# A third plain group ahead of the Strassen groups in each feed-forward

## The chip, the cores and the metric

One Trainium2 chip, one of its cores. The metric is device time in microseconds (us) of one launch, the median of several runs. Engines are named as in the profile: PE (TensorE, the matmuls; PEld is its weight load), DVE (VectorE), ACT (ScalarE), POOL (GpSimd), SP (the queue from which most DMAs are issued).

## The reference, cut to what matters

A step of a two-layer backbone on 640 tokens (512 latent, 128 context) of width 1024. Each layer has two SwiGLU feed-forwards around a token mixer, so there are four feed-forwards in all:

```python
def swiglu(h, w_in, w_out):          # w_in: 1024 x 5632, w_out: 2816 x 1024
    g, u = jnp.split(h @ w_in, 2, axis=-1)
    return (jax.nn.silu(g) * u) @ w_out
...
    for i in range(DEPTH):           # DEPTH = 2
        h = modulate(rms_norm(x, norm_g[i, 0]), mod[:, 0], mod[:, 1])
        x = x + 0.5 * mod[:, 2] * swiglu(h, ffn_w_in[i, 0], ffn_w_out[i, 0])
        ...                          # token mixer
        h = modulate(rms_norm(x, norm_g[i, 2]), mod[:, 6], mod[:, 7])
        x = x + 0.5 * mod[:, 8] * swiglu(h, ffn_w_in[i, 1], ffn_w_out[i, 1])
```

All data are float32. The change concerns only how `h @ w_in` is computed.

## The kernel before, in words

**Precision.** A float32 product is made of three PE matmuls in a reduced float32 format: each operand is split into a high part `hi` (an ACT copy) and a low part `lo` (a DVE subtraction), and PE adds hi*hi, hi*lo and lo*hi in PSUM. In `mm3x` these are lines 695, 696 and 697, each 128x128 weights by 320 columns, that is half of the 640 tokens (`HT`).

**Feed-forward.** The 22 column groups of `w_in` (128 gate and 128 up columns each, one weight tile `raw` of 1 MB) are worked through in three chunks of 6, 8 and 8 groups; after each chunk the second product (`out_proj`) adds its part to `x`. Groups are numbered from 0. Groups 0 and 1 are *plain*: 2 column blocks x 2 token halves x 8 blocks of the inner dimension x 3 = 96 matmuls. From group `NG0` = 2 on, a group is computed by `strassen_in` with the Strassen-Winograd scheme on 2x2 blocks (gate/up, token halves, inner halves): 7 products x 4 x 3 = 84 matmuls.

**What the Strassen groups need besides.** On the weight side, four block sums per group (DVE, lines 289 to 292), and the splits (`split_piece`) of 3.5 tiles' worth of 1024 columns in four pieces, against two pieces of 1024 for a plain group. The S pieces (piece 2 and 3) are split after the sums. On the token side, once per feed-forward, `tbuild`: from the normalised activations, in four pairs of tiles, ACT adds the shift (line 582), DVE makes four block sums (585 to 588), and both split the results into the tiles T (508 on ACT, 509 on DVE): T00 to T03 in the first feed-forward, T20 to T23, T30 to T33 and T50 to T53 in the others, with `ah`, `al`, `bh`, `bl` for the high and low parts. The first product of a Strassen group needs neither S nor T; the second, into the PSUM tile `pg`, needs the S1 block and the T1 part of all four T tiles.

**Start of a feed-forward.** `first_pair` (in the first feed-forward `first_wide`) interleaves groups 0 and 1 with the end of the normalisation, while `tbuild` starts as soon as the last normalised tile is there. Then group 2 follows. Evacuation of a plain group (`fin_half`): per token half a silu on ACT from one PSUM tile (905) and a product on DVE with the other (906), at the end a split (908, 909). A Strassen group has 3 copies on ACT, 3 additions and 2 products on DVE, 2 silus, and the same split.

**Order.** Each engine executes its own rows in the order in which they stand. A list scheduler with priorities sets that order on PE, DVE and ACT; from the first Strassen group on PE keeps the order of the program text (`pe_manual`). Background generators (`tick`) hand out `tbuild`, the splits and the modulation (`ada`) between matmuls. Weights come through a ring of two `raw` tiles, and split pieces through five `whi`/`wlo` buffers; the next weight load is issued when a `raw` tile has been split. A modulation load stands in the same list: four of them ahead of groups 2 to 5 of the first feed-forward, each used by 8 PE products (line 447, 16 matmuls in the trace) into `adaps`, which also takes one of the 8 PSUM tiles.

Of the kernel before, what the change touches and what calls it, by code (L numbers as in the profile page):

```python
# [31 lines left out]
HALVES = ((0, HT), (HT, T))  # L32
SEGS = (((0, HT, 0),), ((HT, TL, 0), (TL, T, 1)))
NS = 47
NG0 = 2
FA = (4, 6, 9, 12, 14, 18)
QD_ = 512
NW = (6, 9)
# [29 lines left out]
def trunk_kernel(  # L68
# [52 lines left out]
    def sbig(name, dt=F32):  # L121
        return ap_.tile([P, T], dt, tag="s", bufs=NS, name=name)

    def stmp(name, dt=F32):
        return ap_.tile([P, T], dt, tag="s", bufs=NS, name=name)
# [5 lines left out]
    def psm(name):  # L131
        return pp.tile([P, 512], F32, tag="b", bufs=8, name=name)
# [18 lines left out]
    def spawn(gen, wait=0):  # L151
        e = [gen, wait]
        bgs.append(e)
        return e
# [40 lines left out]
    for l in range(2):  # L195
        for s in range(2):
            for g in range(KF):
                wtab["fin", l, s, g] = (w_fin[l * 2 + s, g], KD)
                if g >= NG0:
                    stras.add(("fin", l, s, g))  # L200
# [171 lines left out]
    def next_ada():  # L372
        if adae[0] is not None:
            finish(adae[0])
        k = order[st["i"]]
        adae[0] = spawn((ada_v if k[1:] in ADV else ada)(k))
        step(adae[0])
# [5 lines left out]
    def next_group(key):  # L383
        while order[st["i"]][0] == "ada":
            next_ada()
        j = st["i"]
        assert order[j] == key, (order[j], key)
        st["i"] += 1
        return Wt(j)
# [230 lines left out]
    hs = {}  # L620
# [62 lines left out]
    def mm3(o, W, mcol, k, act, hf, start, stop):  # L683
        wh, wl = W.col(k, mcol)
        mm3x(o, wh, wl, *halves(act, hf), start, stop)
# [14 lines left out]
    def mm_fm(o, W, mcol, acts, hf, ks=None):  # L700
        ks = list(range(len(acts))) if ks is None else ks
        for i, k in enumerate(ks):
            mm3(o, W, mcol, k, acts[k], hf, i == 0, i == len(ks) - 1)
# [55 lines left out]
    def first_pair(i, keys, names):  # L759
        if i == 0:  # L760
            yield from first_wide(i, keys, names)
            return
        Ws = [next_group(keys[0])]
        h = hs[i]
        ps = {}
        for hf in range(2):
            if hf == 0:
                for a in range(2):
                    for j in range(2):
                        ps[a, j, 0] = psm(f"{names[a]}{j}0")  # L770
                la[0] = 0
                for k in range(KD):
                    need_h(i, 0, k)
                    for a in range(2):
                        if a == 1 and k == 0:
                            Ws.append(next_group(keys[1]))
                        for j in range(2):
                            mm3(ps[a, j, 0], Ws[a], j, k, h[k], 0, k == 0, k == KD - 1)
                yield ps, 0
            else:  # L780
                for a in range(2):
                    for j in range(2):
                        ps[a, j, 1] = psm(f"{names[a]}{j}1")
                    for k in range(KD):
                        if k == LK:
                            la[0] = 1
                        need_h(i, 1, k)
                        for j in range(2):
                            mm3(ps[a, j, 1], Ws[a], j, k, h[k], 1, k == 0, k == KD - 1)
                    pe_manual(False)  # L790
                    Ws[a].done()
                    yield ps, 1 + a
# [18 lines left out]
    def out_proj(keys, acts, l, gmod, nxt, ks=None):  # L811
        nw = len(keys) if nxt is None else 2
        for gi in range(nw):
            W = next_group(keys[gi])
            for j in range(2):
                for hf in range(2):
                    op_step(keys[gi], W, gi, j, hf, acts, l, gmod, nxt, ks)
                    mid_ada()
            W.done()
        if nw == len(keys):  # L820
            return
        la[0] = 2
        Ws = {}
        end = nxt == len(PHASES)
        for n_, hf in enumerate((1, 0) if end else (0, 1)):
            pe_manual((n_ == 1 or keys[0][0] == "fout") and not end)
            for gi in (2, 3):
                if n_ == 0:
                    Ws[gi] = next_group(keys[gi])
                for j in range(2):  # L830
                    op_step(keys[gi], Ws[gi], gi, j, hf, acts, l, gmod, nxt, ks)
                    mid_ada()
                if n_ == 1:
                    Ws[gi].done()
            chains[nxt, hf] = spawn(norm_chain(nxt, hf, NW[hf]))
# [57 lines left out]
    def ffn(i, l, s, nxt):  # L893
        base = 0
        for ci, n in enumerate(CHUNKS):
            acts = []

            def start_g(g):
                nm = f"a{l}{s}{g}"
                return [sbig(nm + "h", F32R), sbig(nm + "l", F32R), stmp(nm + "s")]  # L900

            def fin_half(e, pg, pu, hf):
                ahi, alo, sg = e
                t0, t1 = HALVES[hf]
                S.activation(out=sg[:, t0:t1], in_=pg[:, :t1 - t0], func=AF.Silu)
                V.tensor_tensor(out=sg[:, t0:t1], in0=sg[:, t0:t1], in1=pu[:, :t1 - t0], op=ALU.mult)
                if hf == 1:
                    S.activation(out=ahi, in_=sg, func=AF.Copy)
                    V.tensor_tensor(out=alo, in0=sg, in1=ahi.bitcast(F32), op=ALU.subtract)

            g0 = base
            if base == 0:
                es = [start_g(0), start_g(1)]
                for ps, stg in first_pair(i, [("fin", l, s, 0), ("fin", l, s, 1)], [f"pf{l}{s}{a}" for a in range(2)]):
                    for a in ((0, 1) if stg == 0 else (stg - 1,)):
                        fin_half(es[a], ps[a, 0, min(stg, 1)], ps[a, 1, min(stg, 1)], min(stg, 1))
                acts += [e[:2] for e in es]
                g0 = 2
            for g in range(g0, base + n):
                e = start_g(g)  # L920
                strassen_in(i, l, s, g, e)
                acts.append(e[:2])
            lastf = nxt if ci == len(CHUNKS) - 1 else None
            if i == 0 and ci == 2:
                spawn(even_tables())
            out_proj([("fout", l, s, ci, g) for g in range(4)], acts, l, 2 if s == 0 else 8, lastf)
            base += n
# [615 lines left out]
    for i, (l, s) in enumerate(PHASES):  # L1543
        if s == 1:
            (even_mixer if l == 0 else odd_mixer)(i, i + 1)
        else:
            ffn(i, l, s // 2, i + 1)
# [108 lines left out]
```

## Time and profile before

| | |
|---|---|
| median of 3 runs | 2505.2 us (2503.99 to 2509.65) |
| the profiled execution's own time | 2501.56 us |
| its span, first to last instruction | 2499.8 us |
| mean granted PE clock | 0.982 of full speed |
| PE busy | 2398.9 us (96% of the span) |
| DVE busy | 1863.5 us (75%) |
| ACT busy | 1077.8 us (43%) |

The profile shows one execution. "Idle before" is the time in which an engine had nothing running ahead of an instruction, with the instruction that released it. [...]

### The profile page before, as it was taken

How to read it: one execution, taken by the hardware profiler on the slowest of the kernel's cores; microseconds unless marked ns; L12 is line 12 of the kernel's file. 1: busy time of each engine (PE TensorE's matmuls, PEld its weight loads, DVE VectorE, ACT ScalarE, POOL GpSimd, SP SyncE). 2: the span in 40 equal slices, each digit the busy share in tenths (PEclk: the TensorE clock that was granted, in tenths of full speed). 3: DMA queues.
4: the chain of work that ended last, by engine and by line, in shares of the span. 5: the costliest groups of instructions: out<-in, count | busy, mean ns of one | idle time of the engine just before them, and what ended most of it. 6: DMA issues, size and time to landing. Idle time of an engine off the chain costs nothing.

```text
span 2499.8 us, 40660 instructions
## 1 busy us (share of the span) xinstructions
PE 2398.9 (96%) x16482; PEld 2341.4 (94%) x16482; DVE 1863.5 (75%) x3785; ACT 1077.8 (43%) x2038; POOL 62.6 (3%) x86
## 2 busy tenths in 40 slices
PE   7899999999899999999999999999999998999998
PEld 6899999899898999999988999999999988999998
DVE  7677767877878777677967786789788877574674
ACT  4525335333326335153542433526767645252452
POOL 1000000000000000000000000001011000000000
PEclk9999999999999999999999999999999999999999
DMA  7342423323241333423224242342111101222121
GB/s 265 114 156 85 150 70 116 135 104 131 71 150 53 129 122 122 152 101 119 85 93 144 102 169 88 116 163 80 41 43 57 54 34 60 76 85 101 68 102 42
DMA packets 44475, 259.30 MB, mean 104 GB/s; under 512 B 5888, under 2 KB 8576, under 8 KB 16768
## 3 DMA queue, kind: packets, MB, share of 16 engines
q1 hardware_dynamic: 41024, 252.37, 28.4%
q8 instruction: 129, 2.11, 0.3%
q0 software_dynamic: 1280, 2.62, 0.3%
q10 hardware_dynamic: 1984, 1.72, 0.2%
q14 instruction: 58, 0.48, 0.1%
HBM read 252.76 MB, written 3.93 MB: 103 GB/s over the span
## 4 chain that ended last, share of the span: by engine, by line
PE 79%; DVE 11%; ACT 3%; DMA 3%; issue 2%; POOL 0%; POOLq 0%; ACTq 0%; DVEq 0%
PE op L696 7%; PE op L697 7%; PE op L695 7%; PE pu L695 7%; PE pu L696 7%; PE pu L697 7%; PE pg L697 4%; PE pg L696 4%; PE pg L695 3%; DVE wlo L309 3%; PE pf L695 2%; PE pf L696 2%; PE pf L697 2%; ACT whi L308 2%; DMA raw<-in_w_fout 1%
## 5 line engine op out<-in xcount | busy, mean ns | idle before, releaser
L309 DVE TENSOR_TENSOR wlo<-raw,whi 128x1024 fp32r<-128x1024 f32 (+1 forms) x488 | 536.1, 1116 | 282.5 <-ACT whi L308 281.4
L308 ACT ACTIVATE whi<-raw 128x1024 fp32r<-128x1024 f32 (+1 forms) x492 | 471.0, 974 | 632.5 <-DMA raw<-in_w_fout 147.8
L807 DVE SCALAR_TENSOR_TENSOR xs<-op,mod,xs 128x128 f32<-128x128 f32 (+2 forms) x312 | 127.1, 436 | 136.9 <-PE op L697 136.5
L524 ACT ACTIVATE nq<-xs 128x320 f32<-128x320 f32 x84 | 39.1, 468 | 132.2 <-DVE xs L807 130.6
L404 DVE SCALAR_TENSOR_TENSOR raw<-raw,sb 128x1024 f32<-128x1024 f32 x72 | 87.6, 1222 | 0.5
L406 DVE CUSTOM_DVE_ANT_0 raw<-raw,sb 128x1024 f32<-128x1024 f32 x72 | 87.5, 1219 | 0.7
L695 PE MATMUL oq<-H4h,whi 128*128 128x320 f32 x256 | 81.1, 318 | 0.2 <-ACT ov L967 0.2
L697 PE MATMUL oq<-H4h,wlo 128*128 128x320 f32 x256 | 79.6, 311 | 0.0
L696 PE MATMUL oq<-H4l,whi 128*128 128x320 f32 x256 | 79.3, 310 | 0.0
L1304 DVE TENSOR_REDUCE amx<-as 128x1 f32<-128x320 f32 x144 | 61.6, 461 | 19.1 <-PE as L1300 18.8
L1312 ACT ACTIVATE ap<-as,anm 128x320 f32<-128x320 f32 x128 | 66.1, 530 | 14.1 <-DVE anm L1307 13.9
L871 ACT COPY p<-pg 128x320 f32<-128x320 f32 x80 | 34.1, 426 | 64.0 <-PE pg L697 63.9
L291 DVE TENSOR_TENSOR raw<-raw 128x512 f32<-128x512 f32 x80 | 55.2, 690 | 1.9
L289 DVE TENSOR_TENSOR raw<-raw 128x512 f32<-128x512 f32 x80 | 55.2, 689 | 1.8
L290 DVE TENSOR_TENSOR raw<-raw 128x512 f32<-128x512 f32 x80 | 54.8, 685 | 0.8
L292 DVE TENSOR_TENSOR raw<-raw 128x512 f32<-128x512 f32 x80 | 54.8, 685 | 0.6
L695 PEld LDWEIGHTS oq<-H4h,whi 128*128 128x128 f32 x256 | 48.1, 188 | 1.3 <-ACT ov L967 0.5
L696 PEld LDWEIGHTS oq<-H4l,whi 128*128 128x128 f32 x256 | 48.1, 188 | 0.4 <-DVE H4l L614 0.3
L697 PEld LDWEIGHTS oq<-H4h,wlo 128*128 128x128 f32 x256 | 48.1, 188 | 0.0
L528 DVE TENSOR_TENSOR nq<-nq,nq 128x320 f32<-128x320 f32 x82 | 40.1, 491 | 9.6 <-ACT nq L524 9.1
L696 PE MATMUL pf<-H3p,whi 128*128 128x320 f32 x144 | 45.4, 316 | 1.8 <-DVE H3p L614 1.8
L696 PE MATMUL pf<-H5p,whi 128*128 128x320 f32 x144 | 44.8, 311 | 2.0 <-DVE H5p L614 2.0
(2715 smaller groups left out, 8899.2 us busy)
## 6 DMA issues: line engine op xcount, KB each, us to landing
raw<-in_w_fin SPq DMA_DIRECT2D x88, 1024.0 KB, 4.7
raw<-in_ada_w SPq DMA_DIRECT2D x64, 1024.0 KB, 4.7
raw<-in_w_fout SPq DMA_DIRECT2D x32, 1024.0 KB, 4.8
raw<-in_w_fout SPq DMA_DIRECT2D x16, 768.0 KB, 4.1
raw<-in_w_oin SPq DMA_DIRECT2D x12, 1024.0 KB, 4.8
raw<-in_w_ein SPq DMA_DIRECT2D x10, 1024.0 KB, 4.9
raw<-in_ada_w SPq DMA_DIRECT2D x32, 256.0 KB, 6.9
raw<-in_w_eout SPq DMA_DIRECT2D x4, 1024.0 KB, 4.9
```

The source lines that it names most:

```text
L289: sub.tensor_tensor(out=a22, in0=a21, in1=a22, op=ALU.add)
L291: sub.tensor_tensor(out=a11, in0=a22, in1=a11, op=ALU.subtract)
L308: S.activation(out=hf, in_=t, func=AF.Copy)
L309: sub.tensor_tensor(out=lf, in0=t, in1=hf.bitcast(F32), op=ALU.subtract)
L404: V.scalar_tensor_tensor(out=o, in0=w, scalar=1.0, in1=sb[:, c * D:(c + 1) * D], op0=ALU.mult, op1=ALU.mult, accum_out=r)
L406: V.tensor_tensor_reduce(out=o, in0=w, in1=sb[:, c * D:(c + 1) * D], scale=1.0, scalar=0.0, op0=ALU.mult, op1=ALU.add, accum_out=r)
L695: PE.matmul(o, wh, xh, start=start, stop=False, skip_group_check=more)
L696: PE.matmul(o, wh, xl, start=False, stop=False, skip_group_check=more)
L697: PE.matmul(o, wl, xh, start=False, stop=stop, skip_group_check=more)
L807: V.scalar_tensor_tensor(out=x[m][:, a:b], in0=ps[:, a - t0:b - t0], scalar=mod[:, l, gmod * KD + m, c:c + 1], in1=x[m][:, a:b], op0=ALU.m ...
L1304: V.tensor_reduce(out=mx[:, j, a:a + 1], in_=sps[j][a][:, 0:w], axis=AX.X, op=ALU.max, negate=True)
L1312: S.activation(out=pj[j][:, a * 320:a * 320 + w], in_=sps[j][a][:, 0:w], func=AF.Exp, bias=b, accum_out=(sm[:, j, a:a + 1] if full else s2 ...
```

## The change

`NG0` becomes 3: group 2 of each feed-forward leaves the set of Strassen groups, and a new loop computes it as a plain group, one token half after the other, ahead of the first Strassen group, which is now group 3.

```diff
-NG0 = 2
+NG0 = 3
...
                 acts += [e[:2] for e in es]
                 g0 = 2
+            while g0 < NG0:
+                es.append(start_g(g0))
+                W = next_group(("fin", l, s, g0))
+                for hf in range(2):
+                    pa = [psm(f"pf{l}{s}{g0}{j}{hf}") for j in range(2)]
+                    for j in range(2):
+                        mm_fm(pa[j], W, j, hs[i], hf)
+                    if hf == 1:
+                        W.done()
+                    fin_half(es[-1], *pa, hf)
+                acts.append(es[-1][:2])
+                g0 += 1
             for g in range(g0, base + n):
                 e = start_g(g)
                 strassen_in(i, l, s, g, e)
```

Over the whole program PE has 15508 rows instead of 15460, DVE 3388 instead of 3424, ACT 1864 instead of 1884, and the DMA issues of SP and POOL stand in the same order as before.

ACT in the first feed-forward, during `tbuild`; `whi11_2` and `whi11_3` are the high parts of group 2's S pieces, `H0t` and `T0` the token side. Before:

```order
L508 ACTIVATE T01ah_621<-H0t1_163 128x640
L308 ACTIVATE whi11_2_776<-raw11_511 128x1024
L508 ACTIVATE T01bh_628<-H0t5_167 128x640
L582 ACTIVATE H0t2_164<-H0t2_164,mod_92 128x512
L582 ACTIVATE H0t2_164<-H0t2_164,mod_92 128x128
L582 ACTIVATE H0t6_168<-H0t6_168,mod_92 128x512
L582 ACTIVATE H0t6_168<-H0t6_168,mod_92 128x128
L308 ACTIVATE whi11_3_825<-raw11_511 128x1024
L508 ACTIVATE T02ah_655<-H0t2_164 128x640
```

and now:

```order
L508 ACTIVATE T01ah_621<-H0t1_163 128x640
L508 ACTIVATE T01bh_628<-H0t5_167 128x640
L582 ACTIVATE H0t2_164<-H0t2_164,mod_92 128x512
L582 ACTIVATE H0t2_164<-H0t2_164,mod_92 128x128
L582 ACTIVATE H0t6_168<-H0t6_168,mod_92 128x512
L582 ACTIVATE H0t6_168<-H0t6_168,mod_92 128x128
L508 ACTIVATE T02ah_655<-H0t2_164 128x640
```

The two S pieces are gone from between the steps of `tbuild`; on DVE, in the same place, the four block sums and the two `wlo` of group 2 are gone too, and the second piece of group 2 is 1024 columns wide instead of 512.

DVE in the fourth feed-forward, at the end of `tbuild`; `wlo206` belongs to group 2, `wlo207` and `raw207` to group 3, `a111` to group 1, `a112` to group 2. Before:

```order
L309 TENSOR_TENSOR wlo206_2_21615<-raw206_21194,whi206_2_21614 128x1024
L509 TENSOR_TENSOR T52al_21680<-H5t2_21238,T52ah_21679 128x640
L309 TENSOR_TENSOR wlo206_3_21717<-raw206_21194,whi206_3_21716 128x1024
L309 TENSOR_TENSOR wlo207_0_21737<-raw207_21416,whi207_0_21736 128x1024
L909 TENSOR_TENSOR a111l_21309<-a111s_21310,a111h_21308 128x640
L509 TENSOR_TENSOR T52bl_21693<-H5t6_21242,T52bh_21692 128x640
L509 TENSOR_TENSOR T53al_21705<-H5t3_21239,T53ah_21704 128x640
L509 TENSOR_TENSOR T53bl_21709<-H5t7_21243,T53bh_21708 128x640
```

and now:

```order
L509 TENSOR_TENSOR T52al_21656<-H5t2_21220,T52ah_21655 128x640
L291 TENSOR_TENSOR raw207_21398<-raw207_21398 128x512
L909 TENSOR_TENSOR a111l_21291<-a111s_21292,a111h_21290 128x640
L509 TENSOR_TENSOR T52bl_21676<-H5t6_21224,T52bh_21675 128x640
L509 TENSOR_TENSOR T53al_21707<-H5t3_21221,T53ah_21706 128x640
L292 TENSOR_TENSOR raw207_21398<-raw207_21398 128x512
L509 TENSOR_TENSOR T53bl_21714<-H5t7_21225,T53bh_21713 128x640
L309 TENSOR_TENSOR wlo207_2_21728<-raw207_21398,whi207_2_21727 128x1024
```

The sums and S pieces that stand among the last T tiles are now those of group 3, and the first S piece comes right behind the last T tile. In the second and third feed-forward the rows move in the same way; there one of the four sums of group 3 stands behind the last T tile.

PE in the second feed-forward, where plain groups end and Strassen begins; `pf01200` to `pf01211` are the plain tiles of group 2, `pu` and `pg` are those of `strassen_in`. Before, the last rows of the first product of group 2 (`pu012`) and the second (`pg012`):

```order
L695 MATMUL pu012_7990<-H2p30_7510,whi86_0_7787 128x320
L696 MATMUL pu012_7990<-H2p30_7510,whi86_0_7787 128x320
L697 MATMUL pu012_7990<-H2p30_7510,wlo86_0_7788 128x320
L695 MATMUL pg012_8010<-T20ah_7881,whi86_2_7892 128x320
L696 MATMUL pg012_8010<-T20al_7882,whi86_2_7892 128x320
L697 MATMUL pg012_8010<-T20ah_7881,wlo86_2_7893 128x320
```

and now, a plain group further on, the same place of group 3:

```order
L695 MATMUL pu013_8103<-H2p30_7504,whi87_0_7961 128x320
L696 MATMUL pu013_8103<-H2p30_7504,whi87_0_7961 128x320
L697 MATMUL pu013_8103<-H2p30_7504,wlo87_0_7962 128x320
L695 MATMUL pg013_8123<-T20ah_7877,whi87_2_8017 128x320
L696 MATMUL pg013_8123<-T20al_7878,whi87_2_8017 128x320
L697 MATMUL pg013_8123<-T20ah_7877,wlo87_2_8018 128x320
```

Group 1's last tile is now followed by 88 rows into `pf01200` to `pf01211` (8 more stand earlier, where 8 rows of `pu012` stood) and 12 into `pu013` before the first row that needs S or T. In the first feed-forward, where group 2 and group 3 have a modulation load each ahead of them, both sets of `adaps` products now stand ahead of group 2; before, the second set stood between groups 2 and 3.

## Rows read from the trace of the kernel before

**Rows 1.** Page, part 1: busy time of the engines, shares, instructions.

```profile
PE 2398.9 (96%) x16482; PEld 2341.4 (94%) x16482; DVE 1863.5 (75%) x3785; ACT 1077.8 (43%) x2038; POOL 62.6 (3%) x86
```

**Rows 2.** Page, part 4: the chain that ended last, shares by engine.

```profile
PE 79%; DVE 11%; ACT 3%; DMA 3%; issue 2%; POOL 0%; POOLq 0%; ACTq 0%; DVEq 0%
```

**Rows 3.** Busy time by stretch: group 2 in the four feed-forwards, six Strassen groups, a wait.

```profile
core 0: us, PE busy (x) PEld busy (x) DVE busy (x) ACT busy (x) POOL busy (x), PEclk, DMA share, GB/s
68.90:91.78 22.88, 17.16 (x118) 14.96 (x116) 15.01 (x24) 12.94 (x22) 0.00 (x0) 0.85 0.22 80
786.55:804.74 18.19, 13.97 (x78) 13.34 (x77) 16.25 (x23) 11.56 (x18) 0.00 (x0) 0.81 0.16 59
1250.44:1270.71 20.27, 15.38 (x78) 14.11 (x77) 14.83 (x21) 10.80 (x17) 0.00 (x0) 0.75 0.14 53
2071.72:2094.07 22.35, 15.15 (x80) 14.23 (x78) 18.20 (x26) 12.34 (x19) 0.00 (x0) 0.77 0.13 47
193.70:267.60 73.90, 73.90 (x506) 73.90 (x505) 57.03 (x85) 38.62 (x62) 0.00 (x0) 1.00 0.25 87
...
766.00:776.00 10.00, 8.21 (x57) 7.95 (x56) 10.00 (x34) 9.34 (x26) 0.00 (x0) 1.00 0.01 2
```

**Rows 4.** PE's waits: fourth feed-forward's group 2; first one's groups 3 to 5; whole run.

```profile
PE pg L696 <- DVE T53al L509: 2.7, 1, 2.7
PE pg L697 <- DVE wlo L309: 2.7, 1, 2.7
PE pg L695 <- ACT whi L308: 1.8, 1, 1.8
...
PE pg L697 <- DVE wlo L309: 2.0, 2, 1.2
...
PE pf L696 <- DVE H2p L614: 1.8, 1, 1.8
```

**Rows 5.** Timeline of PE at three places: start, us, instruction, idle before and releaser.

```profile
74.78 1.94 PE L447 MATMUL adaps<-raw,sc 128*32 128x256 f32 x16 [5.72 <-ACT a000s L905]
...
792.08 0.63 PE L697 MATMUL pg<-T20ah,wlo 128*128 128x320 f32 x1 [2.52 <-DVE wlo L309]
792.51 0.47 PE L695 MATMUL pg<-T21ah,whi 128*128 128x320 f32 x1
792.78 0.47 PE L696 MATMUL pg<-T21al,whi 128*128 128x320 f32 x1
...
817.16 1.07 PE L447 MATMUL adaps<-raw,sc 128*32 128x256 f32 x16
```

**Rows 6.** First copy (line 867) of Strassen groups 7 and 13, first feed-forward.

```profile
L867 ACT COPY a007s<-pu x1: 409/409/409, 193.7 to 193.7; 128x320 f32<-128x320 f32 x1
...
L867 ACT COPY a0013s<-pu x1: 411/411/411, 267.6 to 267.6; 128x320 f32<-128x320 f32 x1
```

**Rows 7.** Groups by line and shape, whole run: count, busy us, mean ns, idle before.

```profile
L309 DVE TENSOR_TENSOR wlo<-raw,whi 128x1024 fp32r<-128x1024 f32 x376 | 451.8, 1220 | 151.5 <-ACT whi L308 150.4
L289 DVE TENSOR_TENSOR raw<-raw 128x512 f32<-128x512 f32 x80 | 55.2, 689 | 1.8
L309 DVE TENSOR_TENSOR wlo<-raw,whi 128x512 fp32r<-128x512 f32 x80 | 55.1, 689 | 111.0 <-ACT whi L308 111.0
...
L881 DVE TENSOR_TENSOR p<-pu,p 128x320 f32<-128x320 f32 x80 | 38.8, 485 | 9.2 <-PE pu L697 9.1
...
L308 ACT ACTIVATE whi<-raw 128x1024 fp32r<-128x1024 f32 x380 | 397.3, 1058 | 447.0 <-DMA raw<-in_w_fin 96.7 <-DVE raw L291 87.0 <-PE op L696 80.6
...
L308 ACT ACTIVATE whi<-raw 128x512 fp32r<-128x512 f32 x80 | 50.1, 626 | 89.9 <-PE pu L696 64.8 <-PE op L696 25.1
```

**Rows 8.** Timeline of ACT at the end of `tbuild`, first feed-forward.

```profile
71.86 0.74 ACT L508 ACTIVATE T03bh<-H0t 128x640 fp32r<-128x640 f32 x1 [0.37 <-DVE H0t L588]
72.50 1.89 ACT L188 ACTIVATE sb<-sb 128x2048 f32<-128x2048 f32 x1
74.30 0.42 ACT L905 ACTIVATE a000s<-pf 128x320 f32<-128x320 f32 x1
```

**Rows 9.** Timeline of DVE: the last T tile in the second, third and fourth feed-forward.

```profile
796.41 0.82 DVE L509 TENSOR_TENSOR T23bl<-H2t,T23bh 128x640 fp32r<-128x640 f32 x1
...
1258.76 0.83 DVE L509 TENSOR_TENSOR T33bl<-H3t,T33bh 128x640 fp32r<-128x640 f32 x1
...
2082.73 0.82 DVE L509 TENSOR_TENSOR T53bl<-H5t,T53bh 128x640 fp32r<-128x640 f32 x1
```

## The prediction

> **What bounds the kernel now.** I read the busy times first: PE is busy 96% of the span, DVE 75%, ACT 43% [rows 1]. Then the chain that ended last: 79% of it is PE, 11% DVE [rows 2]. So the end is set by PE's matmuls, plus the places where PE waits for another engine; what DVE or ACT do beside running matmuls is free. Third, the price of a matmul where nothing waits: six Strassen groups in the first feed-forward take 267.6 - 193.7 = 73.9 us from copy to copy [rows 6], at clock 1.00 [rows 3]; 73.9 / (6 x 84) = 0.1466 us per matmul. Fourth, the place that the change touches: from the last plain matmul of group 1 to the first matmul of group 3, by stretch [rows 3]. The matmuls left of group 2 in them are 84, 76, 76 and 77 (in the last three, 8, 8 and 7 of its rows were run earlier; the counts in the view include one to three rows that overlap an edge, and in the first stretch two sets of `adaps`). What each stretch takes beyond its matmuls is lost:
>
> - first feed-forward: 22.88 - 84 x 0.1466 - 2 sets of `adaps` at 1.07, the one at 817.16 [rows 5] = 8.42 us
> - second: 18.19 - 76 x 0.1466 = 7.05 us
> - third: 20.27 - 11.14 = 9.13 us
> - fourth: 22.35 - 77 x 0.1466 = 11.06 us
>
> Together 35.66 us. Two things make it up. PE waits: in the fourth, 2.7 + 2.7 + 1.8 us for the high and low part of the first S piece and for a T tile [rows 4]; in the first, 5.72 us for a PSUM tile that ACT's silu of group 0 frees, at 74.78 [rows 5]. And after the wait the matmuls run at half speed: two successive starts at 792.51 and 792.78 lie 0.27 us apart instead of 0.147 [rows 5], and the granted clock of the four stretches is 0.85, 0.81, 0.75 and 0.77 against 1.00 [rows 3]. The reader should see one cause: group 2 begins while `tbuild` and the weight sums are still in DVE's queue (16.25 of 18.19 us busy in the second feed-forward, 18.20 of 22.35 in the fourth).
>
> **The change, part by part.** *More matmuls.* Each group 2 has 96 instead of 84, so 48 more: 48 x 0.1466 = 7.04 us, all on PE and on the path. [...]
>
> *Second, third and fourth feed-forward.* PE no longer needs S or T at the end of group 1, but 88 or 89 plain matmuls and the 12 of the next first product later. What must be ready then is the last T tile and group 3's first S piece, so I follow DVE's new order with durations from rows. Ahead of the last T tile there go four sums (4 x 0.69), two S low parts (2 x 1.22), and the second piece of group 2 grows by 1.22 - 0.69 [rows 7]: 2.76 + 2.44 - 0.53 = 4.67 us less. There come group 3's second piece (0.69) and three of its sums (four in the fourth feed-forward): 2.76 or 3.45 us more. So the last T tile, which ended at 797.23, 1259.59 and 2083.55 [rows 9], ends at about 795.3, 1257.7 and 2082.3 on the same scale. Behind it, in the second and third, a sum, a product of group 2 (0.49 [rows 7]) and the S low part (1.22): 797.7 and 1260.1; in the fourth only the S low part: 2083.6. In the second, ACT's high part of it is queued behind the silu of a group 2 tile that PE ends at 786.55 + 64 x 0.1466 = 795.9; with 0.42 [rows 8] and 1.06 [rows 7] the low part then ends at 798.6. PE's first row that reads it stands 102 rows (103 in the fourth) after the start of the stretch: 786.55 + 102 x 0.1466 = 801.5, then 1265.4 and 2086.8. Slack 2.9, 5.3 and 3.2 us. So all three stalls go, with their half-speed matmuls: -27.24 us. If a slack were missed, the price is by the us that it is missed by.
>
> *First feed-forward.* Here the wait is another one: ACT's silu of group 0 stands behind the whole of `tbuild` and a 1.89 us copy [rows 8], and that order stays. But the queue ahead of it gets shorter, on DVE by the same 4.67 us, on ACT by two S high parts less a wider one, 2 x 1.06 - 0.43 = 1.69. `tbuild` goes back and forth between the two, so the silu comes 1.7 to 4.7 us earlier; ACT's own gaps there are released by DVE [rows 8], so I take 4.0. The wait of 5.72 falls to about 1.7 (bounds 1.0 and 4.0). Is the half speed gone as well? Waits of 1.8 us occurred elsewhere and the clock stayed: the one for `H2p` [rows 4], in a stretch at 1.00, that from 766 [rows 3]. So 1.7 of the 8.42 us remain: -6.7 us (bounds -1.7 and -7.4).
>
> *Groups 4 and 5 of the first feed-forward* wait 2.0 us for `wlo` [rows 4], because their weight loads come late. Group 2's tile is now free after two pieces instead of four, the load behind it starts earlier by more than PE is: I take -2.0 us, bounds 0 and -2.0. *New small waits.* In the second feed-forward the last S piece of group 3, which frees the tile for the load of group 4, stands on DVE behind the last product of group 2; the load gains less than PE does. For that and its like I put +1.0 us, bounds 0 and 4 x 1.2 (the longest wait of that kind [rows 4], once per feed-forward). DVE and ACT have less to do per plain group; that is worth nothing where PE runs. DMA issues keep their order.
>
> Sum: 7.04 - 27.24 - 6.7 - 2.0 + 1.0 = -27.9 us. The profiled execution took 2501.56 us (1.76 of it outside the span), so 2473.7; the median of the runs shown is 2505.2, 3.6 above it, so **2477 us**, 1.1% faster. With all terms at their bounds the gain lies between 17.1 and 29.6 us: 2488 and 2476.
>
> **The rivals.** (1) *The first feed-forward gains almost nothing*: ACT bounds `tbuild` there, the wait stays at 4 us and the clock falls all the same. For it: the silu keeps its place in the queue. Against: ACT's gaps. Price 5.0 us, and the 2.0 us of groups 4 and 5 stay: 2484. [...]
>
> (2) *A wait comes back at group 3*: the S piece is later than I compute, because on ACT and DVE it queues behind group 2's evacuation. For it: the new order in the second feed-forward. Against: slacks of 2.9 us and more. Price: a wait like the 2.52 us at 792.08 [rows 5] in three feed-forwards, 7.6 us: 2485.
>
> (3) *Slower*: the whole stall moves on to group 3, since DVE's queue has as much left when Strassen begins. Then 7.04 us are added and nothing is won: 2512. It decides where more than 35.66 - 7.04 = 28.6 us of the stall, 80%, survive; that takes S and T 10 us later, by slack and stall, than the durations give, in each feed-forward. For it: DVE is the busiest engine behind PE, and a plain group has its own split and products. Against: the stretch gets 14.1 us longer on PE and DVE's work ahead of the last T tile gets shorter.
>
> **How the numbers follow.** Forecast 0.75 (2474 to 2481); rival 1 0.12; rival 2 0.08; rival 3 0.04; 0.01 for something between that leaves no measurable difference. Predicted is the likeliest, 2477. The range reaches to rivals 1 and 2 and, below, past the bound by what the runs scatter (2503.99 is 1.2 below their median): 2472 to 2488. A difference under 0.2% (5 us) can't be told from none here. Faster 0.94 (forecast, rivals 1 and 2, less 0.01 for their far ends), same 0.02, slower 0.04.
>
> **What would show it.** In the profile after, in the last three feed-forwards: no wait of `pg` for `wlo`, `whi` or T in the first Strassen group, clock 1.00 in the stretch, and from the last matmul of group 1 to the first of group 3 about 88 x 0.1466 = 12.9 us. In the first: the silu of group 0 near 70.3 instead of 74.30, a wait of `adaps` of about 1.7 us, group 3 starting near 87 instead of 91.78. Wrong would be: a wait of the first `pg` of group 3 over 1 us (rival 2 or 3), a clock below 1.00 behind the wait in the first (rival 1), or plain matmuls of group 2 that wait for their PSUM tiles because silus of group 1 are late.

## The result and the profile after

The median went from 2504.6 us (2501.79 to 2509.65, 4 runs) to **2475.4 us** (2474.71 to 2478.16, 4 runs), ratio 0.9885 with a 95% interval of 0.9872 to 0.9899: 1.0 to 1.3% faster. The forecast was 2477.

The profiled execution of after took 2478.16 us, the slowest of its four runs, while that of before (2501.56) lies just under the fastest of its kernel's runs. So the two traces lie only 23.4 us apart, where the medians lie 29.2 apart, and terms are best compared stretch by stretch.

The page of after, parts 1 and 4, beside [rows 1, 2]:

```profile
PE 2395.3 (97%) x16530; PEld 2342.1 (95%) x16530; DVE 1840.8 (74%) x3749; ACT 1067.4 (43%) x2018; POOL 63.7 (3%) x86
...
PE 80%; DVE 9%; DMA 4%; ACT 4%; issue 2%; POOL 0%; POOLq 0%; ACTq 0%; DVEq 0%
```

PE has 48 matmuls more and is busy 3.6 us less: what it lost before stood in part as busy time, in matmuls at half speed (0.27 us each instead of 0.147 by the prediction's reading of [rows 5]). DVE's share of the chain fell from 11% to 9%.

Busy time by stretch of after, the same places as in [rows 3]: from the last plain matmul of group 1 to the first matmul of group 3, in the four feed-forwards in turn (PEclk is the granted clock, 1.00 at full speed):

```profile
core 0: us, PE busy (x) PEld busy (x) DVE busy (x) ACT busy (x) POOL busy (x), PEclk, DMA share, GB/s
70.49:89.46 18.97, 16.20 (x130) 15.12 (x129) 11.47 (x17) 9.68 (x14) 0.00 (x0) 1.00 0.30 111
784.21:797.12 12.91, 12.91 (x90) 12.91 (x89) 10.08 (x15) 7.36 (x12) 0.00 (x0) 1.00 0.01 1
1241.60:1254.51 12.91, 12.91 (x91) 12.91 (x89) 10.15 (x16) 6.96 (x11) 0.00 (x0) 1.00 0.00 1
2057.18:2070.23 13.05, 13.05 (x91) 13.05 (x90) 11.29 (x17) 6.95 (x11) 0.00 (x0) 1.00 0.01 2
```

The last three are PE busy from end to end, at clock 1.00: 88, 88 and 89 matmuls x 0.1466 us = 12.9, 12.9 and 13.05. Nothing is lost there any more. Against [rows 3] they are 5.28, 7.36 and 9.30 us shorter, 21.94 together, with their 36 additional matmuls in them. In the first a loss remains.

PE's waits in the first feed-forward of after, from 60 to 130 us (engine, line, what was waited for: us in total, times, longest):

```profile
PE adaps L447 <- ACT a000s L905: 2.8, 1, 2.8
PE pg L697 <- DVE wlo L309: 1.1, 1, 1.1
```

The timeline of the same execution there, beside [rows 5, 8]:

```profile
70.50 0.74 ACT L508 ACTIVATE T03bh<-H0t 128x640 fp32r<-128x640 f32 x1 [0.39 <-DVE H0t L588]
71.15 1.89 ACT L188 ACTIVATE sb<-sb 128x2048 f32<-128x2048 f32 x1
72.95 0.42 ACT L905 ACTIVATE a000s<-pf 128x320 f32<-128x320 f32 x1
...
73.42 1.93 PE L447 MATMUL adaps<-raw,sc 128*32 128x256 f32 x32 [2.77 <-ACT a000s L905]
```

The order on ACT is that of before: the last T tile, the silu of `sb`, then the silu that frees a PSUM tile for `adaps`. Only PE's wait is shorter, 2.77 us instead of 5.72. The first feed-forward started 1.6 us later in this execution (70.49 against 68.90), so the silu's place is read from the wait, not from the time on the axis.

### The profile page after: what moved, and what is told of

It is laid out like the page before. It is cut to its first block, busy times and chain, and to the rows that moved or that the text cites. A ratio compares the mean times of both kernels' runs of the same rounds, so it can differ in the third digit from the quotient of the medians.

```text
span 2476.1 us, 40714 instructions
## 1 busy us (share of the span) xinstructions
PE 2395.3 (97%) x16530; PEld 2342.1 (95%) x16530; DVE 1840.8 (74%) x3749; ACT 1067.4 (43%) x2018; POOL 63.7 (3%) x86
## 4 chain that ended last, share of the span: by engine, by line
PE 80%; DVE 9%; DMA 4%; ACT 4%; issue 2%; POOL 0%; POOLq 0%; ACTq 0%; DVEq 0%
PE op L696 8%; PE op L697 8%; PE op L695 8%; PE pu L695 6%; PE pu L696 6%; PE pu L697 6%; PE pg L697 3%; DVE wlo L309 3%; PE pg L696 3%; PE pg L695 3%; PE pf L695 3%; PE pf L696 3%; PE pf L697 3%; ACT whi L308 2%; DMA raw<-in_w_fout 2%
## 5 line engine op out<-in xcount | busy, mean ns | idle before, releaser
L309 DVE TENSOR_TENSOR wlo<-raw,whi 128x1024 fp32r<-128x1024 f32 (+1 forms) x480 | 528.8, 1118 | 286.0 <-ACT whi L308 284.9
L308 ACT ACTIVATE whi<-raw 128x1024 fp32r<-128x1024 f32 (+1 forms) x484 | 465.0, 976 | 639.7 <-DMA raw<-in_w_fout 144.1
L696 PE MATMUL pf<-H5p,whi 128*128 128x320 f32 x172 | 53.8, 313 | 2.0 <-DVE H5p L614 2.0
L696 PE MATMUL pf<-H3p,whi 128*128 128x320 f32 x172 | 53.5, 312 | 1.8 <-DVE H3p L614 1.8
L696 PE MATMUL pf<-H2p,whi 128*128 128x320 f32 x172 | 53.4, 312 | 1.8 <-DVE H2p L614 1.8
L695 PE MATMUL pf<-H0p,whi 128*128 128x320 f32 x172 | 54.3, 318 | 0.2 <-ACT H0p L609 0.2
L696 PE MATMUL pf<-H0p,whi 128*128 128x320 f32 x172 | 53.9, 313 | 0.2 <-DVE H0p L614 0.2
L695 PE MATMUL pf<-H5p,whi 128*128 128x320 f32 x172 | 53.9, 317 | 0.0
L695 PE MATMUL pf<-H3p,whi 128*128 128x320 f32 x172 | 53.8, 317 | 0.0
L695 PE MATMUL pf<-H2p,whi 128*128 128x320 f32 x172 | 53.8, 316 | 0.0
L291 DVE TENSOR_TENSOR raw<-raw 128x512 f32<-128x512 f32 x76 | 52.4, 689 | 1.9
L697 PE MATMUL pf<-H0p,wlo 128*128 128x320 f32 x172 | 53.8, 313 | 0.0
```

Of the source, the lines that this page charges most:

```text
L291: sub.tensor_tensor(out=a11, in0=a22, in1=a11, op=ALU.subtract)
L308: S.activation(out=hf, in_=t, func=AF.Copy)
L309: sub.tensor_tensor(out=lf, in0=t, in1=hf.bitcast(F32), op=ALU.subtract)
L695: PE.matmul(o, wh, xh, start=start, stop=False, skip_group_check=more)
L696: PE.matmul(o, wh, xl, start=False, stop=False, skip_group_check=more)
L697: PE.matmul(o, wl, xh, start=False, stop=stop, skip_group_check=more)
```

## The experiments

Times are medians; the kernel before on the same chip stands beside each.

**The change itself again, and in two halves.** `e0_after_again` is the kernel after. The halves give `NG0` per feed-forward:

```diff
-NG0 = 3
+NG0 = {(0, 0): 3, (0, 1): 2, (1, 0): 2, (1, 1): 2}   # e1; e2 has 2, 3, 3, 3
...
-            while g0 < NG0:
+            while g0 < NG0[l, s]:
```

> The changed kernel itself, timed beside the next three on the same chip. Every theory: 29 us under the kernel before, as its first timing had it.

> The third plain group in the first feed-forward only. Theory (PE waits at the first Strassen group for a queue on DVE and ACT, and only that wait is won): the stretch of the first feed-forward goes from 22.88 to about 19 us as in the profile after, and one of the two waits of groups 4 and 5 goes, together 4.9 us under the kernel before. Rival (a plain group is cheaper anywhere, since it has less work for DVE and ACT): a quarter of the whole, 7.3 us.

> The third plain group in the second, third and fourth feed-forward only. Theory: 5.3 + 7.4 + 9.3 = 21.9 us under the kernel before, each the stall of its stretch less 1.76 us for 12 more matmuls, and the first stretch stays at 22.9 us. Rival (the feed-forwards depend on each other through the weight loads, so parts don't add up): this and the run with the first alone differ from the whole by more than 3 us in sum.

Before: 2507.7. Measured: e0 2477.6, ratio 0.9881 (0.9867 to 0.9896). e1 2502.9, 0.9982 (0.9970 to 0.9995): -4.5 us by the ratio. e2 2483.5, 0.9905 (0.9892 to 0.9917): -23.8 us. The halves add to -28.3, the whole gives -29.8. So the last three feed-forwards carry five sixths of it, where the forecast's terms gave them four fifths. In e2's trace PE has no wait at group 3 in these three, and the wait of `adaps` in the first is 5.73 us, as before. The times of the halves do not settle every rival: e1's interval reaches from 1.3 to 7.5 us, so it holds both the 4.9 that were expected and the rival's 7.3. What speaks against a plain group that is cheaper anywhere is e3 below.

In e1 the first feed-forward came out worse than in after. Its stretch, by busy time:

```profile
68.35:89.10 20.75, 17.77 (x130) 16.16 (x129) 11.70 (x18) 9.67 (x14) 0.00 (x0) 0.92 0.28 102
```

PE's timeline of e1 behind the wait:

```profile
71.49 2.61 PE L447 MATMUL adaps<-raw,sc 128*32 128x256 f32 x32 [2.98 <-ACT a000s L905]
...
74.47 0.47 PE L696 MATMUL pf<-H0p,whi 128*128 128x320 f32 x1
...
75.53 0.47 PE L697 MATMUL pf<-H0p,wlo 128*128 128x320 f32 x1
```

And the same instructions in e0:

```profile
73.95 1.93 PE L447 MATMUL adaps<-raw,sc 128*32 128x256 f32 x32 [2.77 <-ACT a000s L905]
...
76.06 0.31 PE L696 MATMUL pf<-H0p,whi 128*128 128x320 f32 x1
...
76.64 0.31 PE L697 MATMUL pf<-H0p,wlo 128*128 128x320 f32 x1
```

The last two rows are four matmuls apart: 0.145 us each behind a wait of 2.77 us, 0.265 us each behind one of 2.98 us. With the longer wait, that costs e1 1.8 us (20.75 against 18.97). This is what the first rival feared of the clock; in the profiles of the whole change it did not happen (clock 1.00).

**One plain group more.**

```diff
-NG0 = 3
+NG0 = 4
```

> Four plain groups ahead of Strassen in each feed-forward. Theory: no stall is left to win in the last three, so 48 more matmuls cost 48 x 0.1466 = 7.0 us; in the first the one wait left in group 5 may go (1.3): 5.7 to 7.0 us over the changed kernel, 22 to 23 under the kernel before. Rival (less work for DVE and ACT is what counts): again faster than the changed kernel, by up to as much as the first step.

2487.3 us, ratio 0.9923 (0.9910 to 0.9936): about 10 us slower than e0 by the medians, 6.0 than after by the spans of the two profiles (2482.1 and 2476.1). The sign is as expected, 5.7 to 7.0 us being the expected size: with no stall left to cover, a plain group costs its 12 matmuls. The profile also shows two waits that after has not, each of a later Strassen group, in the second feed-forward and in the third:

```profile
PE pu L695 <- DVE p L881: 1.8, 1, 1.8
...
PE pu L695 <- DVE p L881: 1.6, 1, 1.6
```

Why they arise, and how much of the difference they make, isn't shown.

**Leaving the weight sums of group 2 out.**

```diff
-            if h == 2:
+            if h == 2 and key[3] > 2:
```

> The kernel before, with the four block sums of group 2's weights left out in each feed-forward (4 x 0.69 = 2.76 us of DVE; the S pieces are then split from the raw blocks, so that part of the computation is changed). Theory (DVE's queue is what PE waits for): each stall gets shorter by about 2.8 us and some half speed with it, 8 to 16 us under the kernel before. Rival (PE waits for loads or PSUM tiles, DVE only stands last in the list): no change within 2 us.

2498.8 us against 2508.1, ratio 0.9971 (0.9958 to 0.9983): -7 us by the ratio, -9 by the medians, around the lower edge of the 8 to 16 that were expected. The three stretches:

```profile
785.29:804.82 19.53, 16.14 (x78) 14.59 (x77) 13.95 (x21) 10.16 (x17) 0.00 (x0) 0.74 0.16 55
1247.94:1266.64 18.70, 14.80 (x78) 13.44 (x77) 14.62 (x22) 10.12 (x17) 0.00 (x0) 0.82 0.15 57
2071.43:2089.52 18.09, 14.48 (x80) 13.37 (x78) 14.01 (x21) 9.57 (x16) 0.00 (x0) 0.81 0.17 58
```

Against [rows 3] they change by +1.34, -1.57 and -4.26 us, and the clock still falls. So the sums are a part of the queue, not the whole stall: PE still waits for the low parts of the T tiles, in the third feed-forward 2.1, 0.8 and 1.0 us:

```profile
PE pg L696 <- DVE T32al L509: 2.1, 1, 2.1
PE pg L696 <- DVE T33al L509: 1.0, 1, 1.0
PE pg L696 <- DVE T31al L509: 0.8, 1, 0.8
```

Taking 2.8 us of DVE's work away buys 4.5 us in three stretches. The change moves PE's need 14 us back and takes 1.2 to 1.9 us of DVE's work from ahead of the last T tile; together they remove the 27 us of loss.

**Cover without need.** `e7_dummies` and `e8_dummies_24` put 48 and 24 unused matmuls into group 2 of the last three feed-forwards of the kernel before, in front of S1 x T1:

```diff
+        if g == 2 and i > 0:
+            pd = psm("pd" + nm)
+            for kk in range(16):          # e8: range(8)
+                xh, xl = xq["B11"](kk % 4)
+                wh, wl = W.prod("A11", kk % 4)
+                mm3x(pd, wh, wl, xh, xl, True, True)
```

> The kernel before, with 48 extra matmuls (7.04 us, into a PSUM tile that nobody reads) behind the first product of group 2 in the last three feed-forwards, so that PE runs where it waited. Theory (of the 27.2 us lost there some 11 are matmuls at half speed behind the wait): the stretches become about 18.2, 18.2 and 20.3 us, 4 us under the kernel before though 21.1 us of useless matmuls are added. Rival (the half speed costs nothing that the wait doesn't cost already): the added matmuls outlast the waits of 4.2, 4.8 and 7.2 us, and the kernel is 5 us slower.

> The kernel before, with 24 matmuls (3.5 us) of unused results instead of 48 in front of S1 x T1 in group 2 of the last three feed-forwards. Theory A (TensorE's clock falls as soon as waits of two to five microseconds remain): the last T tile sets the end as before, waits of about 2.1, 2.8 and 5.4 us remain in front of the T3 tiles, the clock still falls, and the stretches from the last matmul of group 1 to the first of group 3 stay at 18.2, 20.3 and 22.4 us; time as before within 1 us. Theory B (the longer cover saves the clock although waits remain): stretches 18.2, 18.0 and 20 us or less, 4 us or more faster than the kernel before, as much as with 48. Rival (any matmul added is paid in full, since the waits are behind it and not in front): 3.5 us more per stretch, 10 us slower.

e7 took 2501.7 us against 2508.1, ratio 0.9984 (0.9974 to 0.9994). Its stretches:

```profile
788.15:806.33 18.18, 18.18 (x126) 18.18 (x125) 15.66 (x22) 11.44 (x18) 0.00 (x0) 1.00 0.18 59
1249.07:1268.26 19.19, 18.45 (x127) 18.18 (x125) 16.24 (x23) 11.15 (x17) 0.00 (x0) 1.00 0.17 55
2072.57:2091.23 18.66, 18.44 (x127) 18.18 (x125) 15.72 (x22) 10.91 (x17) 0.00 (x0) 1.00 0.18 58
```

Each has 7.04 us of work that nobody needs, and each stretch is as long as before or shorter (18.19, 20.27 and 22.35 in [rows 3]), 4.8 us in sum (18.2, 18.2 and 20.3 were expected). The work itself was free, it lay in the wait; the gain is the clock, 1.00 instead of 0.81, 0.75 and 0.77. This shows the two halves of the loss apart: the wait, and the half-speed matmuls that it leaves behind.

With 24 (e8):

```profile
783.75:801.92 18.17, 15.45 (x102) 14.66 (x101) 16.25 (x23) 11.58 (x18) 0.00 (x0) 1.00 0.17 59
1246.23:1267.86 21.63, 17.89 (x103) 17.14 (x101) 16.38 (x23) 11.18 (x18) 0.00 (x0) 0.84 0.14 49
2069.84:2090.20 20.36, 16.87 (x103) 16.38 (x102) 16.89 (x24) 10.94 (x17) 0.00 (x0) 0.92 0.15 53
```

Neither theory came out whole. As theory A says, the clock fell where a wait of 3.1 us remained in front of T33 and T53; in the second feed-forward, with waits of at most 1.0 us, it did not. But the waits are not the 2.1, 2.8 and 5.4 us that it computed, the third stretch is 1.3 us longer than its 20.3, the fourth 2.0 shorter than its 22.4, and the run is not as before. Theory B has the sign of the run, not the stretches. In sum the stretches gained 0.65 us. The whole run, 2498.0 us against 2508.1, ratio 0.9962 (0.9950 to 0.9974), gained far more than these stretches explain. Its profiled execution lies 3.7 us under that of before; where the rest comes from stays open.

**A product moved ahead.** In group 2 of the kernel before, A12 x B21, which needs no T, goes ahead of S1 x T1:

```diff
         S.copy(out=g1, in_=pu[:, :HT])
+        if g == 2:
+            pf = psm("pf" + nm)
+            product(pf, "A12", "B21")
         pg = psm("pg" + nm)
```

> The kernel before, with the product of group 2 that needs neither S nor T (A12 with B21) moved ahead of the first one that does. It adds no matmul and takes no work from DVE; PE only comes 12 matmuls, 1.76 us, later to the first S piece. Theory (what counts is how late PE comes against how long DVE's queue is): at least 1.76 us less stall in each of the last three feed-forwards, 5.3 us, with less half speed up to 8, under the kernel before. Rival (only DVE's shorter queue counts): 0.

2511.1 us against 2508.1, ratio 1.0012 (1.0001 to 1.0023): the theory failed. The stretches:

```profile
792.16:809.52 17.36, 13.81 (x78) 12.54 (x77) 16.46 (x23) 11.32 (x18) 0.00 (x0) 0.90 0.18 62
1256.96:1278.47 21.51, 15.71 (x79) 14.55 (x77) 15.53 (x22) 10.69 (x17) 0.00 (x0) 0.76 0.14 50
2083.65:2104.44 20.79, 14.01 (x79) 12.84 (x77) 16.50 (x23) 10.80 (x17) 0.00 (x0) 0.84 0.14 51
```

PE's waits in the second of them:

```profile
PE pg L696 <- DVE T33al L509: 2.6, 1, 2.6
PE pg L695 <- ACT T33ah L508: 1.5, 1, 1.5
PE pu L695 <- ACT a102s L877: 1.2, 1, 1.2
```

And the timeline at the last of these waits:

```profile
1269.97 1.06 ACT L308 ACTIVATE whi<-raw 128x1024 fp32r<-128x1024 f32 x1 [1.73 <-PE pu L696]
1270.93 0.41 ACT L877 COPY a102s<-pu 128x320 f32<-128x320 f32 x1
...
1271.39 0.63 PE L695 MATMUL pu<-T30ah,whi 128*128 128x320 f32 x1 [1.24 <-ACT a102s L877]
```

Two reasons can be read. The product is 12 matmuls, 1.76 us, far less than the 7 to 11 us lost in a stretch, so waits remain and the clock falls anyway (0.90, 0.76 and 0.84). And it had been cover already: it stood between S2 x T2 and S3 x T3, which share the PSUM tile `pu`, while ACT copied the tile out. With the product gone from there, PE waits for that copy, which itself is queued behind a weight split. So the three stretches gained 1.15 us in sum, and the first feed-forward has the new wait too (0.5 us). The two profiles lie 10.4 us apart (2511.95 and 2501.56), the medians 3; most of the 10.4 is not in these stretches, and 2.1 of it is in a place that the last section shows.

**The silu of `sb` out of the way.** Line 188 moves behind the silus of groups 0 and 1, in the kernel after (e5, e10) and in the kernel before (e9):

```diff
-        S.activation(out=sb, in_=sb, func=AF.Silu)
...
                 acts += [e[:2] for e in es]
+                if i == 0:
+                    S.activation(out=sb, in_=sb, func=AF.Silu)
```

> The changed kernel, with the 1.89 us silu of the conditioning vector on ACT moved behind the evacuation of groups 0 and 1 in the first feed-forward. Theory (that silu and the T steps ahead of it hold back the PSUM tile for which PE waits 2.9 us): 1.9 us under the changed kernel, 31 under the kernel before, and the wait of adaps about 1.0 us. Rival (another instruction holds the tile, or the silu is missed later by the modulation): 0.

> The kernel before, with the silu of sb (1.89 us on ScalarE) moved behind the silus of groups 0 and 1 in the first feed-forward, and no third plain group. Theory A (the silu of sb delays a000s, and with it the sums over adaps, by its own length): the wait of adaps goes from 5.72 to about 3.9 us, the stretch from the last plain matmul to group 3 from 22.88 to 21.0 us, the run 1.9 us faster. Theory B (the shorter wait also spares part of the half-speed matmuls behind it): 19 to 20 us, 3 to 4 us faster. Rival (something else, T03 or a copy of weights, is as late as the silu): wait and stretch within 0.5 us of before, no gain.

> The kernel after with the silu of sb moved behind the silus of the first pair, once more, beside the kernel after on the same chip. Theory (the silu costs PE its 1.77 us of the first feed-forward's stretch, and what hid it in the first timing was the scatter of a later output product, 57.6 to 61.7 us): stretch 17.2 us again, median 1 to 3 us under that of the kernel after. Rival (what is won there is lost again behind it, each time): stretch 17.2 us, output product of the first chunk again near 61.7 us, median within 1 us of the kernel after or above it.

> The kernel after, unchanged, as the partner of the run with the late silu. Both theories: ratio to the kernel before within 0.987 to 0.990, stretch of the first feed-forward 18.97 us if the wait of adaps (2.8 us) leaves the clock at full speed, about 20.7 us if the clock falls as it did with the third plain group in the first feed-forward alone.

e9: the wait of `adaps` fell from 5.72 to 3.95 us, and the stretch to 20.17 us. Busy time by stretch:

```profile
69.40:89.57 20.17, 16.22 (x118) 14.69 (x117) 14.97 (x25) 11.10 (x21) 0.00 (x0) 0.92 0.24 93
```

The timeline of PE:

```profile
73.52 1.07 PE L446 MATMUL adaps<-raw,sc 128*32 128x256 f32 x16 [3.95 <-ACT a000s L904]
```

That is 2.7 us less than the 22.88 of [rows 3], between the two theories; the run took 2505.5 us against 2508.1, ratio 0.9991 (0.9981 to 1.0001), which can't be told from no gain. The silu does delay `adaps`, by about its own length (1.77 of 1.89 us); but the wait of 3.95 us behind it is `tbuild`'s, and half-speed matmuls still follow (clock 0.92 in the stretch).

On top of the change (e5, then e10), the stretch of 18.97 us became 17.20 and 16.69. The one of e10:

```profile
69.96:86.65 16.69, 16.21 (x130) 15.12 (x129) 10.82 (x17) 7.40 (x13) 0.00 (x0) 1.00 0.33 127
```

The wait of `adaps` there fell from 2.77 to 1.0 and 0.5 us. The times: e5 2478.4 (ratio 0.9882, 0.9869 to 0.9895) beside 2477.6 of e0 (0.9881), which ran on another chip; e10 2475.7 (0.9871, 0.9855 to 0.9888) beside 2478.0 of e11, the kernel after (0.9885, 0.9869 to 0.9901; its stretch 18.99 us). So the place gains 1.8 to 2.3 us each time, and the medians differ by +0.8 and -2.3 us; the 1.9 us that were expected of e5 did not show in its run. The rival of e10, that the gain is lost again behind it each time, is out: the output product that took 61.67 us in e5 took 57.73 in e10. Whether the run is faster can't be told at this scatter.

## Why the prediction was right

*The last three feed-forwards* (-27.24 for the stalls, with 36 x 0.1466 = 5.28 us of added matmuls in them: net -21.96) measured -21.94. The computed ends of DVE's queue held closely enough. In the second feed-forward the low part of the S piece was to end 798.6 - 786.55 = 12.05 us after the stretch's start; on DVE's timeline of after the last T tile, and behind it the split that waited for ACT:

```profile
791.25 0.81 DVE L509 TENSOR_TENSOR T23bl<-H2t,T23bh 128x640 fp32r<-128x640 f32 x1
...
795.22 1.23 DVE L309 TENSOR_TENSOR wlo<-raw,whi 128x1024 fp32r<-128x1024 f32 x1 [2.16 <-ACT whi L308]
```

795.22 + 1.23 - 784.21 = 12.24 us. PE's row that reads it comes 102 matmuls after the start, at 14.95, so 2.7 us of slack remain where 2.9 were computed. In the third and fourth the same split of group 3 stands at:

```profile
1249.92 1.21 DVE L309 TENSOR_TENSOR wlo<-raw,whi 128x1024 fp32r<-128x1024 f32 x1
...
2066.24 1.22 DVE L309 TENSOR_TENSOR wlo<-raw,whi 128x1024 fp32r<-128x1024 f32 x1
```

It ends 9.5 and 10.3 us after the start of its stretch, where 9.7 and 11.9 were computed.

*Half speed* belongs to the loss, and where the waits go it goes too: e7 shows it by itself (clock 1.00 in its three stretches, where before had 0.81, 0.75 and 0.77). The step that was to show that a wait of 1.7 us leaves the clock alone does not hold. It took one of three waits of the same length, that for `H2p`; in the same trace of before the one for `H3p` has matmuls at half speed behind it. The waits, and the 5 us behind each:

```profile
771.35 0.41 PE L696 MATMUL pf<-H2p,whi 128*128 128x320 f32 x1 [1.79 <-DVE H2p L614]
...
1233.69 0.42 PE L696 MATMUL pf<-H3p,whi 128*128 128x320 f32 x1 [1.78 <-DVE H3p L614]
...
771.35:776.35 5.00, 5.00 (x34) 5.00 (x35) 5.00 (x17) 5.00 (x14) 0.00 (x0) 1.00 0.01 3
1233.69:1238.69 5.00, 5.00 (x23) 5.00 (x24) 5.00 (x17) 5.00 (x14) 0.00 (x0) 0.66 0.01 3
```

*The first feed-forward* was mis-sized: its loss, 18.97 - 96 x 0.1466 - 2.14 = 2.76 us, is 5.66 below the 8.42 of before, not 6.7. I took the silu to come 4.0 us earlier; the wait of `adaps` fell by 5.72 - 2.77 = 2.95 us, inside the bounds of 1.7 to 4.7, and the remaining wait is 2.8 instead of 1.7 us. By the rows above, a wait of 1.7 us would not have made the clock sure either. That the clock stays was right in the three profiles of the kernel after (after, e0, e11) and in that of e3, wrong in e1, where the same instructions stand at this place. So this part of the forecast had the right outcome, and luck in it.

*Groups 4 and 5 of the first feed-forward*: -2.0 us was forecast, one of the two waits for `wlo` went, 2.0 to 1.1 us: -0.9.

*New small waits* (+1.0): none shows in the four stretches, nor in the Strassen groups behind them up to the first output product, beyond the 1.1 us just named.

The stretches and that wait sum to -21.94 - 3.91 - 0.9 = -26.8 us. The forecast's -27.9 comes to -28.9 without its allowance for new waits, so the terms are 2.1 us off, nearly all of it in the first feed-forward.

That the forecast came within 2 us of the median is closer than this account can vouch for. Against the terms' 26.8 us the medians lie 29.2 apart and the spans of the two profiles 23.7 (2499.8 and 2476.1). Part of the profiles' shortfall is scatter outside the stretches: the first feed-forward starts 1.6 us later, and the wait of 1.78 us for `H2p`, which left the clock at 1.00 in before, is followed by half speed in after, as is the one for `H5p`; from either of these waits to the start of the stretch behind it, after takes 1.5 us longer than before. The 5 us behind the wait for `H2p` in after, beside the rows of before above:

```profile
767.48:772.48 5.00, 5.00 (x23) 5.00 (x24) 5.00 (x17) 5.00 (x14) 0.00 (x0) 0.66 0.00 0
```

*The rivals.* The first is half right: the wait stays close to 3 us, but the clock fell in one of the five profiles of this place only. The second and third are out: no wait of `pg` for S or T at group 3, in any of the four feed-forwards. Rival 3's argument, that DVE is as late as before, falls by the measured end of the split above.

## What to carry to other kernels

When an engine stalls because the inputs of a cheaper algorithm are late, price the stall as wait plus the half-speed matmuls behind it, then compare it with the extra work of running the plain algorithm a little longer: here 7 us of additional matmuls bought back 33 us of lost time. Stop as soon as the stall is gone: one step more (e3) cost 6 to 10 us. A wait that remains may have half-speed matmuls behind it in one run and not in the next, here 1.5 us each time, so compare stretches before totals. Before moving an independent product forward as cover, look at what it covers where it stands (e6).

## What the runs showed of the hardware

**The clock behind a wait.** The same instructions behind a wait of 2.77 us (e0, after) and of 2.98 us (e1) ran at 0.145 and 0.265 us per matmul; behind 2.83 us in e3 they ran at full speed (0.147). There the longest of the waits is the one with half speed behind it, but the length of a wait does not decide alone. The waits for `H2p`, `H3p` and `H5p` are about 1.78 us long in all fourteen profiles, with PE busy and the clock at 1.00 for 5 us before; in 25 of these 42 cases about a dozen matmuls at half speed follow, in 17 none. In the 5 us from the end of the wait the clock is 1.00 for `H2p` and `H5p` and 0.66 for `H3p` in before, and 0.66 for all three in after. A wait of 2.6 to 2.8 us in the second feed-forward (the first Strassen group behind the first output product, with another of 0.4 to 0.7 us shortly after) was followed by half speed in all fourteen (in the 5 us from its end the clock is 0.66 in before and 0.74 in after). What decides between the cases stays open here.

**Scatter from one place.** The output product of the second chunk of the first feed-forward (384 matmuls, at 0.1466 us each 56.3 us; the expectation of e10 calls it the first chunk's) has the same matmuls in all fourteen profiles, and took 57.6 to 61.7 us. Busy time by stretch in after:

```profile
273.63:331.25 57.62, 56.58 (x387) 56.32 (x385) 42.15 (x73) 10.58 (x11) 0.00 (x0) 1.00 0.36 128
```

The same in e5:

```profile
270.71:332.38 61.67, 58.37 (x386) 57.88 (x385) 42.59 (x73) 10.58 (x11) 0.00 (x0) 0.97 0.35 121
```

And PE's waits in that stretch of e5:

```profile
PE op L694 <- ACT a0013h L889: 2.2, 1, 2.2
PE op L695 <- DVE a0013l L890: 1.1, 1, 1.1
```

PE reaches the last group's activations a little before they are split. Nine profiles have a wait for the high part as well as for the low one; in three of them (e0, e5 and e6) ten to twelve matmuls at half speed follow (in e6 the clock is 0.50 from 286.50 to 288.50 us), in the other six, before with 1.1 and 1.1 us among them, the clock stays at 1.00. In e9 the third and the fourth feed-forward had it too (61.55 and 60.22 us for the same kind of block). Such a place moves a run by up to 4 us and hides an edit worth 2 us, like the late silu.
